# A two-layer fp32 model on one core: three gathered groups of tokens instead of two, and a routing step in another place

## The chip, the cores and the metric

The kernel runs on one core of a Trainium2 chip. The metric is the device time of one execution in microseconds (us). Engines are named as in the profile: PE (TensorE matmul), PEld (its weight loads), DVE (VectorE), ACT (ScalarE), POOL (GpSimd) and SP (SyncE, which here only issues transfers). DMA means the core's 16 DMA engines.

## The reference

The input is 512 tokens of width 1024, with 16 meta tokens ahead of them. The first block mixes them (convolution and latent attention) and then applies a feed-forward layer of experts. That layer is what the change touches:

```
q = (xb @ wq).reshape(C, 8 heads, 2, 64);  s = einsum('chpd,hpnd->chpn', q, keys)   # 128 keys per half
sv, si = top_k(s, 16)                                   # per head and half
top_s, sel = top_k((sv[:, :, 0, :, None] + sv[:, :, 1, None, :]).reshape(C, 8, 256), 16)
eidx = 16 of 128*128 experts per head;  g = softmax(top_s)
act = gelu(einsum('chkd,cd->chk', u_tab[eidx], xb))     # 8 * 16 = 128 experts per token
out = einsum('chk,chkd->cd', g * act, v_tab[eidx])
```

A second block follows (a gated convolution, a feed-forward layer, sparse attention, a feed-forward layer). All is computed in fp32 precision: a product of two fp32 matrices is made of three matmuls of high and low parts.

## The kernel before, in words

The layer of experts is computed in two ways. For the last 96 tokens the rows of `u_tab` and `v_tab` are **gathered** (groups of 64 and 32 tokens, `GROUPS`, line 60). For the other 416 (`TD`) it is computed **dense**: U times x for all 16384 experts, in 128 chunks of 128 experts, multiplied by a matrix G that holds the gates (zero for experts not chosen), and then V. A chunk of U is 24 matmuls of 128x128 weights and `TD` columns (lines 269 to 272); a V piece is 12 (lines 260 to 262), and a pass over half of a run's V is 8 pieces.

The order of the work on each engine is the order in which the program emits it (`manual_schedule`); nothing is planned by a tool.

**Stage A (352 to 830 us).** PE computes 84 chunks of U ahead (`ahead`), whose activations go to DRAM. Beside it DVE does the routing, a generator that yields charges; after each chunk it is advanced until the chunk's budget `BUD` is used up. The tokens lie in four tiles of 128, worked on in the order 3, 0, 1, 2. For each tile `route` ranks (`top16`, two heads at a time, 7.7 units, four times), decodes the indices to expert numbers (13.4 units), yields one more `BUD`, and lets PE transpose the result (`pt`, line 1078). For tile 3 it first computes `eg` and calls `pick` (line 921), which spreads the gathered tokens' indices and gates over the partitions. Then `onehots` builds one-hot matrices for 16 tokens on DVE (4 instructions, 6.7 units), and `build_g` multiplies them on PE, which ACT copies out and writes to `gd` in DRAM. There are `NSB` = 26 such blocks, 2 of them in tile 3. On ACT stand the casts of U to its high part (`wh`, line 119) and, in the decoding, an Exp; POOL subtracts to get the low part of U (`wl`, line 121).

**Gather steps.** `gstep` advances a second generator, `gathered`: each step loads one tile of 128 rows (512 KB) two steps ahead by an indirect DMA on POOL (line 935, three buffers), and takes one product on DVE: with x and a sum along the row for U (line 949), or times a factor and added to an accumulator for V (line 958). 64 tokens need 64 + 64 steps, 32 tokens 32 + 32. At the end of a group PE folds the accumulator (line 963). In stage A two chunks of six have a step, for which 1.9 units are charged.

**Stage B (850 to 1640 us).** 16 runs of 8 chunks. In each, G's part is loaded (`load_g`, POOL's queue), products and their high and low parts are made (`w_prod`, `w_split`), and two V passes follow (`v_pass`, accumulators `d`). Between the passes come the 44 fresh chunks of U, with one gather step each; `GV` lists after which of its 8 pieces a V pass takes a step. V is split by ACT and DVE two pieces ahead, with four buffers. What is left of the gather steps is done before the last V pass.

Of the kernel before, what the change touches and what calls it, by code (L numbers as in the profile page):

```python
# [9 lines left out]
F32 = mybir.dt.float32  # L10
# [33 lines left out]
AHEAD = 5  # L44
EXTRA = 4
PRE = 2
BUD = 5.0
NA = 4
NB = 1
ND = 2  # L50
# [39 lines left out]
OJ = (((), (0,), ()), ((1,), (), (2, 3)))  # L90
PF = 5
PA = tuple(range(6))
GV = (1, 2, 4, 6)


class Stream:
# [45 lines left out]
def _body(tc, nc, V, S, PE, GP, A, out, upto, tap, ctx):  # L142
# [99 lines left out]
    def col(name, i=0):  # L242
        p, n = COLS[name]
        return cols[:, p + i:p + i + 1]
# [100 lines left out]
    def xtile(p, h="xh", l="xl", n=8, c=T, bufs=None):  # L345
        return p.tile([128, n, c], F32R, name=h, bufs=bufs), p.tile([128, n, c], F32R, name=l, bufs=bufs)
# [429 lines left out]
    with ExitStack() as st:  # L776
        with st0 as st1:
            with ExitStack() as st2:
# [61 lines left out]
                xg = xq.tile([128, len(GROUPS), 8, 128], F32, name="xg")  # L840
# [20 lines left out]
                def norm_x(k):  # L861
                    tn = xq.tile([128, T], F32, name="tn", bufs=2)
                    V.scalar_tensor_tensor(tn, H[k], col("g_ffn", k), rB[:, :T], op0=OP.mult, op1=OP.mult)
                    split(xnh[:, k], xnl[:, k], tn, None)
                    for a, (t0, n, P) in enumerate(groups):
                        V.tensor_copy(xg[:, a, k].rearrange("p (b t) -> p b t", b=P),
                                      tn[:, None, t0:t0 + n].to_broadcast([128, P, n]))

                for h in range(8):
                    w = ws.get()  # L870
# [16 lines left out]
                for a, (t0, n, P) in enumerate(groups):  # L887
                    V.tensor_copy(dup[:, a].rearrange("p (b t) -> p b t", b=P),
                                  ident[:, None, t0 - 384:t0 - 384 + n].to_broadcast([128, P, n]))
                    xt.append(gx.tile([128, 1024], F32, name="xt", bufs=len(GROUPS)))  # L890
# [19 lines left out]
                S.activation(a, ps, AF.Gelu)  # L910
                return a

            gix = gx.tile([128, len(GROUPS), 64], U32, name="gix")
            gga = gx.tile([128, len(GROUPS), 64], F32, name="gga")
            gdt = gx.tile([128, len(GROUPS), 64], F32, name="gdt")

            def pick(eg):

                for a, (t0, n, P) in enumerate(groups):
                    ps = bank()  # L920
                    PE.matmul(ps[:, :256], lhsT=dup[:, a], rhs=eg.rearrange("p a n -> p (a n)"), start=True, stop=True)
                    m = 128 // P
                    for b in range(P):
                        r = slice(b * n, b * n + n)
                        V.tensor_copy(gix[r, a, :m], ps[r, b * m:b * m + m])
                        V.tensor_copy(gga[r, a, :m], ps[r, 128 + b * m:128 + b * m + m])

            def gathered():

                todo = [(a, v, j) for a, (t0, m, P) in enumerate(groups) for v in (0, 1) for j in range(128 // P)]  # L930
                tiles = []

                def load(a, v, j):
                    g = gx.tile([128, 1024], F32, name="row", bufs=GB)
                    GP.indirect_dma_start(out=g, out_offset=None, in_=A["vr" if v else "ur"],  # L935
                                          in_offset=bass.IndirectOffsetOnAxis(ap=gix[:, a, j:j + 1], axis=0))
                    tiles.append(g)

                for t in todo[:GB - 1]:
                    load(*t)  # L940
                yield
                for n, (a, v, j) in enumerate(todo):
                    if n + GB - 1 < len(todo):
                        load(*todo[n + GB - 1])
                    g = tiles.pop(0)
                    t0, m, P = groups[a]
                    L = 128 // P
                    if not v:
                        V.scalar_tensor_tensor(g, g, 1.0, xt[a], op0=OP.mult, op1=OP.mult,
                                               accum_out=gdt[:, a, j:j + 1])  # L950
                        if j == L - 1:
                            S.activation(gdt[:, a, :L], gdt[:, a, :L], AF.Gelu)
                            V.tensor_tensor(gdt[:, a, :L], gdt[:, a, :L], gga[:, a, :L], op=OP.mult)
                    elif j == 0:
                        gac[a] = gx.tile([128, 1024], F32, name="xt", bufs=len(GROUPS))
                        V.tensor_scalar(gac[a], g, gdt[:, a, 0:1], None, op0=OP.mult)
                    else:
                        V.scalar_tensor_tensor(gac[a], g, gdt[:, a, j:j + 1], gac[a], op0=OP.mult, op1=OP.add)  # L958
                    yield
                    if v and j == L - 1:  # L960
                        ps = bank()
                        for k in range(8):
                            PE.matmul(ps[:, k * m:(k + 1) * m], lhsT=gac[a][:, k * 128:(k + 1) * 128],
                                      rhs=fold[:, a, :m], start=True, stop=True)
# [3 lines left out]
            fold = gx.tile([128, len(GROUPS), 64], F32, name="fold")  # L968
            for a, (t0, n, P) in enumerate(groups):
                V.tensor_reduce(fold[:, a, :n], ident.rearrange("p (b t) -> p t b", b=P), op=OP.add, axis=AX.X)  # L970
            gat, gac = [], {}

            def gstep(n=1):
# [17 lines left out]
            def route(i):  # L991

                sv = wk.tile([128, 8, 2, 16], F32, name="sv", bufs=1)
                si = wk.tile([128, 8, 2, 16], U32, name="si", bufs=1)
                ts = wk.tile([128, 8, 16], F32, name="ts", bufs=1)
                tp = wk.tile([128, 8, 16], U32, name="tp", bufs=1)
                for h in range(0, 8, 2):
                    ch = []
                    for u in range(4):
                        tmp = wk.tile([128, 128], F32, name="tmp", bufs=4)  # L1000
# [17 lines left out]
                        ch.append((ts[:, h + u], tp[:, h + u], c, tmp[:, :112]))  # L1018
                    top16(ch)
                    yield 3.0  # L1020

                tpf = tp.rearrange("p h k -> p (h k)")
                ii = wk.tile([128, 8, 128], U32, name="ol")[:, :4]
# [42 lines left out]
                yield BUD  # L1066
                if i == 3:
                    eg = wk.tile([128, 2, 128], F32, name="eg", bufs=1)
# [61 lines left out]

# [29 lines left out]
        def load_g(r):  # L1160
            if r < len(runs):
                gt[r] = pk.tile([128, NSB, RUN, SUB], F32, name="gt", bufs=2)
                for b in range(0, NSB, NSB // GP_):
                    sl = slice(b, b + NSB // GP_)
# [740 lines left out]
```

## Time and profile before

| | |
|---|---|
| median of 3 runs | 2871.4 us (2870.38 to 2872.52) |
| the profiled execution | 2870.35 us, span 2868.2 us |
| PE busy | 2758.8 us (96%) in 14308 matmuls |
| DVE busy | 1905.4 us (66%) |
| ACT busy | 1193.5 us (42%) |
| POOL busy | 876.0 us (31%) |
| mean granted clock of PE | 0.982 |
| DMA | 457.17 MB, mean 159 GB/s |

The shares are means over stages with different limits. A matmul's end is modelled, so PE's pace is read from the distance between starts.

### The profile page before, as it was taken

To read this page: it belongs to the slowest core of one execution; us is meant where nothing else is said; L and a number is where in the kernel's file an instruction comes from. 1 tells how busy PE (TensorE), PEld (TensorE's weight loads), DVE (VectorE), ACT (ScalarE), POOL (GpSimd) and SP (SyncE) were. 2 spreads that over 40 slices of the span, in tenths; PEclk is the share of its full clock that TensorE was granted. 3 is DMA by queue.
4 is the path that set the end of the run, shared out by engine and by line. 5 is a ranking of instruction groups with operands and counts; after the bars stand their busy time and mean duration, and the time that the engine had idled before them with its cause. 6 is when DMAs were issued, how large, how long until landed. Compare 5 with 4: busy or idle time off the path is not lost. (4 is left out here: it accounts for less than half of the span.)

```text
span 2868.2 us, 38216 instructions
## 1 busy us (share of the span) xinstructions
PE 2758.8 (96%) x14308; PEld 2429.1 (85%) x14308; DVE 1905.4 (66%) x3477; ACT 1193.5 (42%) x1962; POOL 876.0 (31%) x521
## 2 busy tenths in 40 slices
PE   8778998999999999999999999999999999999998
PEld 7646898999989999999999988888887866788887
DVE  5887599798957867777778765444436489544433
ACT  5564543646553333343333423332223378433322
POOL 3653155555534456564456000000003133000000
PEclk9889999999999999999999999999999999999999
DMA  3102255767678888888888333333234200233332
GB/s 126 52 8 66 70 175 179 262 193 259 211 278 305 285 295 281 306 283 280 294 296 301 99 101 96 96 97 100 91 101 141 81 23 1 74 99 100 96 94 83
DMA packets 156568, 457.17 MB, mean 159 GB/s; under 512 B 17056, under 2 KB 40864, under 8 KB 152800
## 3 DMA queue, kind: packets, MB, share of 16 engines
q1 hardware_dynamic: 103008, 273.33, 29.5%
q0 software_dynamic: 36704, 135.54, 14.2%
q10 hardware_dynamic: 16672, 45.88, 4.0%
q8 instruction: 112, 1.84, 0.3%
q14 instruction: 72, 0.59, 0.1%
HBM read 407.43 MB, written 47.25 MB: 159 GB/s over the span
## 5 line engine op out<-in xcount | busy, mean ns | idle before, releaser
L119 ACT CAST wh<-wr 128x1024 fp32r<-128x1024 f32 (+1 forms) x356 | 369.4, 1038 | 394.4 <-issue 206.3
L121 DVE TENSOR_TENSOR wl<-wr,wh 128x1024 fp32r<-128x1024 f32 (+1 forms) x231 | 287.5, 1245 | 368.1 <-ACT wh L119 363.4
L121 POOL TENSOR_TENSOR wl<-wr,wh 128x1024 fp32r<-128x1024 f32 x125 | 334.0, 2673 | 330.2 <-ACT wh L119 325.4
L262 PE MATMUL m<-xh,wl 128*128 128x512 f32 x1080 | 422.2, 391 | 3.4 <-POOL wl L121 2.7
L260 PE MATMUL m<-xh,wh 128*128 128x512 f32 x1080 | 424.4, 393 | 0.0
L261 PE MATMUL m<-xl,wh 128*128 128x512 f32 x1048 | 407.9, 389 | 0.0
L269 PE MATMUL m<-xh,wh 128*128 128x416 f32 x1024 | 365.0, 356 | 9.7 <-ACT stg L1115 5.8
L261 PE MATMUL d<-wtl,vh 128*128 128x416 f32 x1024 | 359.5, 351 | 2.6 <-DVE wtl L253 2.6
L260 PE MATMUL d<-wth,vh 128*128 128x416 f32 x1024 | 359.8, 351 | 1.8 <-DVE hT L1206 0.9
L270 PE MATMUL m<-xl,wh 128*128 128x416 f32 x1024 | 360.9, 352 | 0.0
L262 PE MATMUL d<-wth,vl 128*128 128x416 f32 x1024 | 359.1, 351 | 0.2
L121 DVE TENSOR_TENSOR vl<-vr,vh 128x512 fp32r<-128x512 f32 x256 | 174.7, 688 | 140.1 <-ACT vh L119 133.9
L262 PEld LDWEIGHTS m<-xh,wl 128*128 128x128 f32 x1080 | 203.2, 188 | 49.4 <-DVE wl L121 3.4
L260 PEld LDWEIGHTS m<-xh,wh 128*128 128x128 f32 x1080 | 203.2, 188 | 43.3 <-issue 1.2
L119 ACT CAST vh<-vr 128x512 fp32r<-128x512 f32 x256 | 153.9, 619 | 206.1 <-DMA vr<-in_vr 148.5
L261 PEld LDWEIGHTS m<-xl,wh 128*128 128x128 f32 x1048 | 196.8, 188 | 41.2 <-issue 1.0
L935 POOL DMA_INDIRECT row<-in_vr,gix x96 | 174.6, 1818 | 141.0 <-DVE xt L958 109.3
L272 PE MATMUL m<-xh,wl 128*128 128x416 f32 x1024 | 213.3, 350 | 0.0
L910 ACT ACTIVATE act<-m 128x416 f32<-128x416 f32 x128 | 66.4, 519 | 343.3 <-PE m L272 336.5
L269 PEld LDWEIGHTS m<-xh,wh 128*128 128x128 f32 x1024 | 194.9, 190 | 15.8 <-ACT stg L1115 10.2
L261 PEld LDWEIGHTS d<-wtl,vh 128*128 128x128 f32 x1024 | 192.3, 188 | 5.5 <-DVE wtl L253 3.8
L260 PEld LDWEIGHTS d<-wth,vh 128*128 128x128 f32 x1024 | 192.2, 188 | 5.1 <-ACT act L910 1.3
(428 smaller groups left out, 5378.5 us busy)
## 6 DMA issues: line engine op xcount, KB each, us to landing
wr<-in_u SPq DMA_DIRECT2D x128, 512.0 KB
vr<-in_vr SPq DMA_DIRECT2D x256, 256.0 KB
wr<-in_w_gu SPq DMA_DIRECT2D x88, 512.0 KB
gd<-stg ACTq DMA_DIRECT2D x26, 1024.0 KB
gt<-gd POOLq DMA_DIRECT2D x32, 832.0 KB
ad<-act ACTq DMA_DIRECT2D x84, 208.0 KB
act<-ad SPq DMA_DIRECT2D x84, 208.0 KB
wr<-in_w_down SPq DMA_DIRECT2D x32, 512.0 KB
```

What stands on the lines that cost most here:

```text
L119: nc.scalar.copy(hi[:, :n], t[:, :n])
L121: eng.tensor_tensor(lo[:, :n], t[:, :n], hi[:, :n].bitcast(F32), op=OP.subtract)
L260: PE.matmul(ps, lhsT=wh, rhs=xh, start=first, stop=False)
L261: PE.matmul(ps, lhsT=wh, rhs=xl, start=False, stop=False)
L262: PE.matmul(ps, lhsT=wl, rhs=xh, start=False, stop=last)
L269: PE.matmul(ps, lhsT=wh, rhs=xhs[k], start=k == 0, stop=False)
L270: PE.matmul(ps, lhsT=wh, rhs=xls[k], start=False, stop=False)
L272: PE.matmul(ps, lhsT=w[1][:, wc + k * 128:wc + k * 128 + 128], rhs=xhs[k], start=False, stop=k == n - 1)
L910: S.activation(a, ps, AF.Gelu)
L935: GP.indirect_dma_start(out=g, out_offset=None, in_=A["vr" if v else "ur"], in_offset=bass.IndirectOffsetOnAxis(ap=gix[:, a, j:j + 1], axi ...
```

## The change

The tokens 400 to 415, dense before, form a third gathered group of 16 (P = 8: each token has 8 partitions, 16 + 16 more steps). `TD` is 400 and `NSB` 25; all matmuls of U and V have 400 columns. The third group's x is made late, inside the gather steps (`late_x`: eight products on DVE, eight transposes on PE, two copies on ACT), and `pick` folds its indices by a mask and seven adds, instead of copies from ranges of partitions. `GV` has five entries. `route` is cut in three: `rank`, `decode`, `turn`. The next tile's first ranking (heads 0 and 1) comes between a tile's `decode` and its `turn`, its other three after the tile's one-hots; the idle charge of one `BUD` after a decoding is 1.0. `BUD` is 4.9.

```diff
-BUD = 5.0
+BUD = 4.9
-GROUPS = ((64, 2), (32, 4))
+GROUPS = ((64, 2), (32, 4), (16, 8))
-GV = (1, 2, 4, 6)
+GV = (1, 2, 4, 5, 7)
...
-                xnh, xnl = xtile(xp)
+                xnh, xnl = xtile(xp, c=TD)
...
+                    if n % 32:
+                        x = wk.tile([128, 2, P, m], F32, name="o0", bufs=1)
+                        V.tensor_tensor(x, ps[:, :256].rearrange("p (z b j) -> p z b j", z=2, b=P),
+                                        own[:, None, :, None].to_broadcast([128, 2, P, m]), op=OP.mult)
+                        for b in range(1, P):
+                            V.tensor_tensor(x[:, :, 0], x[:, :, 0], x[:, :, b], op=OP.add)
+                        V.tensor_copy(gix[a], x[:, 0, 0])
+                        V.tensor_copy(gga[a], x[:, 1, 0])
+                        continue
...
+                def late_x(a):
+                    t0, m, P = groups[a]
+                    xs = gx.tile([128, 8, 128], F32, name="row", bufs=GB)
+                    for k in range(8):
+                        V.scalar_tensor_tensor(xs[:, k].rearrange("p (b t) -> p b t", b=P),
+                                               H[k][:, None, t0:t0 + m].to_broadcast([128, P, m]), col("g_ffn", k),
+                                               rB[:, None, t0:t0 + m].to_broadcast([128, P, m]),
+                                               op0=OP.mult, op1=OP.mult)
+                    xt.append(gx.tile([128, 1024], F32, name="xt", bufs=2))
+                    for z in range(2):
+                        ps = bank()
+                        for k in range(4):
+                            PE.transpose(ps[:, k * 128:(k + 1) * 128], xs[:, 4 * z + k], ident)
+                        S.copy(xt[a][:, 512 * z:512 * z + 512], ps)
...
                 for n, (a, v, j) in enumerate(todo):
+                    if len(xt) == a:
+                        late_x(a)
...
             def routing():
                 late = []
-                for i in (3, 0, 1, 2):
-                    tk = yield from route(i)
+                tiles = (3, 0, 1, 2)
+                yield from rank(3, range(0, 8, 2))
+                for n, i in enumerate(tiles):
+                    id01 = yield from decode(i)
+                    nxt = tiles[n + 1] if n < 3 else None
+                    if nxt is not None:
+                        yield from rank(nxt, (0,))
+                    tk = yield from turn(i, id01)
                     for s in range(min(8, NSB - 8 * i)):
                         a = yield from onehots(tk, s)
                         late.append((i, s) + a)
                         if len(late) > 1:
                             build_g(*late.pop(0))
+                    if nxt is not None:
+                        yield from rank(nxt, range(2, 8, 2))
```

## Rows read from the trace of the kernel before

**Rows 1.** Windows: length, busy of PE, PEld, DVE, ACT, POOL, PEclk, DMA share, GB/s.

```profile
488.00:622.00 134.00, 127.69 (x836) 123.63 (x835) 112.99 (x283) 71.50 (x87) 73.32 (x32) 0.98 0.67 227
900.00:1400.00 500.00, 499.92 (x2662) 495.81 (x2661) 368.29 (x521) 180.19 (x305) 277.79 (x161) 1.00 0.84 288
1400.00:1580.00 180.00, 180.00 (x958) 178.66 (x957) 140.31 (x198) 64.99 (x113) 95.34 (x53) 1.00 0.88 299
```

**Rows 2.** Waits of PE, 352:830: engine line <- releaser: us, times, longest.

```profile
PE m L1078 <- DVE id L1060: 9.6, 3, 4.9
...
PE m L269 <- ACT wh L119: 3.8, 2, 3.3
PE m L1113 <- ACT stg L1115: 2.8, 3, 2.3
PE m L921 <- DVE eg L1070: 2.4, 1, 2.4
PE m L1078 <- DVE id L1065: 2.3, 3, 1.6
```

**Rows 3.** Timeline of PE (start, length): steady 416, 512 and 256 columns.

```profile
1112.01 0.35 PE L261 MATMUL d<-wtl,vh 128*128 128x416 f32 x1
...
1113.90 0.35 PE L262 MATMUL d<-wth,vl 128*128 128x416 f32 x1
...
333.45 0.39 PE L260 MATMUL m<-xgh,wh 128*128 128x512 f32 x1
...
336.20 0.39 PE L260 MATMUL m<-xgh,wh 128*128 128x512 f32 x1
...
2840.84 0.28 PE L260 MATMUL m<-ah,wh 128*128 128x256 f32 x1
...
2841.42 0.28 PE L262 MATMUL m<-ah,wl 128*128 128x256 f32 x1
```

**Rows 4.** Groups by line: busy us, mean ns | idle before.

```profile
L269 PE MATMUL m<-xh,wh 128*128 128x416 f32 x1024 | 365.0, 356 | 9.7 <-ACT stg L1115 5.8 <-ACT wh L119 3.8
```

**Rows 5.** Timeline of DVE: a ranking's start and the next's, a decoding.

```profile
446.23 0.44 DVE L981 MAX8 ts<-cand 128x8 f32<-128x112 f32 x2
...
455.21 0.27 DVE L981 MAX8 ts<-cand 128x8 f32<-128x112 f32 x1
...
472.56 5.79 DVE L1059 TENSOR_TENSOR o<-o 128x1024 f16<-128x1024 f16 x3
478.38 0.29 DVE L1060 TENSOR_TENSOR id<-o 128x128 f32<-128x128 f16 x1
```

**Rows 6.** Timeline of POOL in that decoding.

```profile
475.34 2.40 POOL L121 TENSOR_TENSOR wl<-wr,wh 128x1024 fp32r<-128x1024 f32 x1 [0.55 <-ACT wh L119]
```

**Rows 7.** Timeline of PE: the pick matmuls.

```profile
408.81 2.08 PE L921 MATMUL m<-eg,dup 128*128 128x256 f32 x4 [2.45 <-DVE eg L1070]
```

**Rows 8.** Groups by line: the longest of the four one-hot instructions.

```profile
L1101 DVE TENSOR_TENSOR ol<-o,tk 128x2048 f16<-128x2048 f16 x26 | 47.1, 1812 | 0.0
```

**Rows 9.** Groups by line, DVE, 900 to 1600 us: a gather step.

```profile
L958 DVE SCALAR_TENSOR_TENSOR xt<-row,gdt,xt 128x1024 f32<-128x1024 f32 x94 | 127.4, 1355 | 6.3 <-DMA row<-in_vr,gix 6.2
```

**Rows 10.** Timeline of a V pass: DVE's split, PE's first use of it.

```profile
1111.92 0.69 DVE L121 TENSOR_TENSOR vl<-vr,vh 128x512 fp32r<-128x512 f32 x1
...
1113.33 0.35 PE L262 MATMUL d<-wth,vl 128*128 128x416 f32 x1
```

**Rows 11.** Timeline: transposes of x; before the last V pass, DVE and PE.

```profile
349.06 0.98 PE L893 MATMUL d<-ident,xg 128*128 128x128 f32 x7
...
1594.99 2.17 DVE L1206 TENSOR_TENSOR hT<-d,hT 128x832 f32<-128x832 f32 x2 [2.25 <-PE d L262]
...
1595.93 1.87 PE L963 MATMUL m<-fold,xt 128*128 128x32 f32 x16
```

**Rows 12.** Waits of POOL, 825 to 850 us.

```profile
POOL gt L1165 <- DMA gd<-stg: 24.2, 1, 24.2
```

**Rows 13.** Waits of PE, 850 to 900 us.

```profile
PE d L261 <- DVE wtl L253: 2.6, 4, 1.3
```

More of the change, by code (lines that the diff above doesn't have):

```diff
@@ L837, in _body @@
                     return dump()
-                xnh, xnl = xtile(xp)
+                xnh, xnl = xtile(xp, c=TD)
                 gx = pool(st, "gx", side="right")
-                xg = xq.tile([128, len(GROUPS), 8, 128], F32, name="xg")
+                xg = xq.tile([128, 2, 8, 128], F32, name="xg")
                 groups = []
@@ L863, in norm_x @@
                     V.scalar_tensor_tensor(tn, H[k], col("g_ffn", k), rB[:, :T], op0=OP.mult, op1=OP.mult)
-                    split(xnh[:, k], xnl[:, k], tn, None)
+                    split(xnh[:, k], xnl[:, k], tn[:, :TD], None)
                     for a, (t0, n, P) in enumerate(groups):
-                        V.tensor_copy(xg[:, a, k].rearrange("p (b t) -> p b t", b=P),
-                                      tn[:, None, t0:t0 + n].to_broadcast([128, P, n]))
+                        if a < 2:
+                            V.tensor_copy(xg[:, a, k].rearrange("p (b t) -> p b t", b=P),
+                                          tn[:, None, t0:t0 + n].to_broadcast([128, P, n]))
                 for h in range(8):
@@ L889, in _body @@
                                   ident[:, None, t0 - 384:t0 - 384 + n].to_broadcast([128, P, n]))
-                    xt.append(gx.tile([128, 1024], F32, name="xt", bufs=len(GROUPS)))
+                    if a == 2:
+                        break
+                    xt.append(gx.tile([128, 1024], F32, name="xt", bufs=2))
                     ps = bank("d")
@@ L911, in u_chunk, with parts @@
                 return a
-            gix = gx.tile([128, len(GROUPS), 64], U32, name="gix")
-            gga = gx.tile([128, len(GROUPS), 64], F32, name="gga")
-            gdt = gx.tile([128, len(GROUPS), 64], F32, name="gdt")
+            def parts(name, dt, sizes):
+                t = gx.tile([128, sum(sizes)], dt, name=name)
+                return [t[:, sum(sizes[:a]):sum(sizes[:a + 1])] for a in range(len(sizes))]
+            gix = parts("gix", U32, [128 // P for _, _, P in groups])
+            gga = parts("gga", F32, [128 // P for _, _, P in groups])
+            gdt = parts("gdt", F32, [128 // P for _, _, P in groups])
             def pick(eg):
@@ L935, in load @@
                     GP.indirect_dma_start(out=g, out_offset=None, in_=A["vr" if v else "ur"],
-                                          in_offset=bass.IndirectOffsetOnAxis(ap=gix[:, a, j:j + 1], axis=0))
+                                          in_offset=bass.IndirectOffsetOnAxis(ap=gix[a][:, j:j + 1], axis=0))
                     tiles.append(g)
+                def late_x(a):
[6 more added lines that the diff above has]
+                                               op0=OP.mult, op1=OP.mult)
+                    xt.append(gx.tile([128, 1024], F32, name="xt", bufs=2))
+                    for z in range(2):
[3 more added lines that the diff above has]
+                        S.copy(xt[a][:, 512 * z:512 * z + 512], ps)
                 for t in todo[:GB - 1]:
@@ L949, in gathered @@
                         V.scalar_tensor_tensor(g, g, 1.0, xt[a], op0=OP.mult, op1=OP.mult,
-                                               accum_out=gdt[:, a, j:j + 1])
+                                               accum_out=gdt[a][:, j:j + 1])
                         if j == L - 1:
-                            S.activation(gdt[:, a, :L], gdt[:, a, :L], AF.Gelu)
-                            V.tensor_tensor(gdt[:, a, :L], gdt[:, a, :L], gga[:, a, :L], op=OP.mult)
+                            S.activation(gdt[a], gdt[a], AF.Gelu)
+                            V.tensor_tensor(gdt[a], gdt[a], gga[a], op=OP.mult)
                     elif j == 0:
-                        gac[a] = gx.tile([128, 1024], F32, name="xt", bufs=len(GROUPS))
-                        V.tensor_scalar(gac[a], g, gdt[:, a, 0:1], None, op0=OP.mult)
+                        gac[a] = gx.tile([128, 1024], F32, name="xt", bufs=2)
+                        V.tensor_scalar(gac[a], g, gdt[a][:, 0:1], None, op0=OP.mult)
                     else:
-                        V.scalar_tensor_tensor(gac[a], g, gdt[:, a, j:j + 1], gac[a], op0=OP.mult, op1=OP.add)
+                        V.scalar_tensor_tensor(gac[a], g, gdt[a][:, j:j + 1], gac[a], op0=OP.mult, op1=OP.add)
                     yield
@@ L963, in gathered @@
                             PE.matmul(ps[:, k * m:(k + 1) * m], lhsT=gac[a][:, k * 128:(k + 1) * 128],
-                                      rhs=fold[:, a, :m], start=True, stop=True)
+                                      rhs=fold[a], start=True, stop=True)
                         h = hT[:, :, M0 + t0:M0 + t0 + m]
                         V.tensor_tensor(h, ps[:, :8 * m].rearrange("p (k t) -> p k t", k=8), h, op=OP.add)
-            fold = gx.tile([128, len(GROUPS), 64], F32, name="fold")
+            fold = parts("fold", F32, [n for _, n, P in groups])
             for a, (t0, n, P) in enumerate(groups):
-                V.tensor_reduce(fold[:, a, :n], ident.rearrange("p (b t) -> p t b", b=P), op=OP.add, axis=AX.X)
+                V.tensor_reduce(fold[a], ident.rearrange("p (b t) -> p t b", b=P), op=OP.add, axis=AX.X)
+            own = gx.tile([128, 8], F32, name="own")
+            V.tensor_reduce(own, ident.rearrange("p (b t) -> p b t", b=8), op=OP.add, axis=AX.X)
             gat, gac = [], {}
@@ L989, in top16, with rank @@
                     V.max_index(di[:, 8:16], dv[:, 8:16], tmp)
[L991 to L997, printed above, removed]
+            rk = {}
+            def rank(i, heads):
+                if 0 in heads:
+                    rk[i] = (wk.tile([128, 8, 2, 16], F32, name="sv", bufs=1),
+                             wk.tile([128, 8, 2, 16], U32, name="si", bufs=1),
+                             wk.tile([128, 8, 16], F32, name="ts", bufs=1),
+                             wk.tile([128, 8, 16], U32, name="tp", bufs=1))
+                sv, si, ts, tp = rk[i]
+                for h in heads:
                     ch = []
@@ L1065, in route, with turn @@
                 V.tensor_tensor(ge, ge, gs[:, 1, :, None].to_broadcast([128, 8, 16]), op=OP.mult)
-                yield BUD
+                yield 1.0
+                return id01
+            def turn(i, id01):
                 if i == 3:
-                    eg = wk.tile([128, 2, 128], F32, name="eg", bufs=1)
+                    eg = wk.tile([128, 8, 128], F32, name="o1")[:, :2]
                     V.scalar_tensor_tensor(eg[:, 0], id01[:, 0], 128.0, id01[:, 1], op0=OP.mult, op1=OP.add)
@@ L1162, in load_g @@
                 gt[r] = pk.tile([128, NSB, RUN, SUB], F32, name="gt", bufs=2)
-                for b in range(0, NSB, NSB // GP_):
-                    sl = slice(b, b + NSB // GP_)
+                m = -(-NSB // GP_)
+                for b in range(0, NSB, m):
+                    sl = slice(b, min(b + m, NSB))
                     nc.gpsimd.dma_start(gt[r][:, sl].rearrange("p b i t -> p b (i t)"),
```

6 lines of the change are left out of this document (4 added, 2 removed).

## The prediction

> **What bounds the kernel now.** I read the windows first, to see which engine is full in which stage. From 900 to 1400 us (V passes with fresh U chunks between them) PE is busy 499.92 of 500 us, and the same holds to 1580 [rows 1]: PE alone sets this stage, while DVE has a fifth to a quarter of its time free and the DMA engines are at 0.84 to 0.88. In the stage before (352 to 830 us: 84 ahead chunks of U beside the routing on DVE) PE has holes, 6.31 us in tile 1's period [rows 1]. PE's waits of that stage name them [rows 2]: transposes that wait for the decoding (9.6 + 2.3), a weight cast on ACT behind an Exp that waits for DVE (3.8), the last one-hot blocks (2.8), and the pick matmul for `eg` (2.4). Nothing after 1640 us is touched.
>
> **What 16 columns are worth.** In steady state matmuls with 416 columns start 1.89 us apart for 10 steps, 0.189 each; with 512 columns 2.75 for 12, 0.229; with 256 columns 0.58 for 5, 0.116 [rows 3]. Between 256 and 512 a column costs 0.44 ns, and 416 lies within 5 ns of that line; I take 6.85 ns for 16 columns (2.4 GHz alone gives 6.7). Six groups of 1024 such matmuls (one of them is [rows 4]) are 6144: 42.1 us of PE. The 44 fresh chunks of 24 and the 3072 matmuls of the V passes lie in the stage that PE fills: 4128 x 6.85 ns = **28.3 us** off the path. The 84 ahead chunks hold the other 13.8: a chunk falls from 24 x 0.188 = 4.52 us to 4.36.
>
> The Trainium skill (TensorE: Matmul & The Clock Gate, Back-to-back issue gap) has the spacing set by weight load and matmul together, 81 ns at N=128 and 131 at N=512; by that slope 16 columns would be an estimated 2.1 ns, and all 6144 matmuls worth 12.8 us. The trace's 0.229 us at 512 disagrees with that page, and the measurement decides.
>
> **The routing stage.** Tile 1's period of 134 us, less 24 chunks of 4.52, 4.5 of waits and 1 for transposes, leaves 2.5 us for each of its 8 one-hot blocks. PE's own work changes by -13.8 (columns), -2.5 (one block fewer) and +1.0 (a third pick matmul, by the 2.08 us of two [rows 7]): -15.3. But its waits change too; there I follow program order.
> - Tile 3. `eg` is computed in `turn`, so on DVE it now stands behind the ranking of tile 0's first two heads. Such a ranking took 8.98 us, with a gather step in it [rows 5]; I take 8.5. By the code's charges (52.9 units and five gather charges of 1.9, made although nothing is gathered yet, at 4.9 a chunk) the pick comes after 13 chunks instead of 12: PE arrives 13 x 4.36 - 12 x 4.52 = 2.4 us later. The wait for `eg`, 2.45 us [rows 7], becomes 2.45 + 8.5 - 2.4 = **8.6**, +6.1.
> - Tile 0 has the longest waits for decoding and cast, 4.9 + 3.3 = 8.2 [rows 2]. From pick to transposes PE has 12 chunks instead of 14 and a block: 13.4 less. DVE has one one-hot block less (four instructions of at most 1.8 us [rows 8], say 6), one ranking less (8.5), and 1.8 more to fold the third group (ten copies and adds, each under the 0.29 of a 128x128 add [rows 5]): 12.7 less. Then 8.2 + 13.4 - 12.7 = 8.9, +0.7.
> - Tiles 1 and 2 have the rest of those waits: 9.6 + 2.3 + 3.8 - 8.2 = 7.5. A tile now has 23 chunks between its transposes and the last ones, not 24. In tile 1's period DVE is busy 113 of 134 us [rows 1]; PE's work falls to 23 x 4.36 + 8 x 2.5 + 1 = 121. If the one-hots still wait for PE as today, the decoding is ready a ranking (8.5) earlier against a PE that comes some 6 earlier, and the waits fall to about 5. If DVE never waits in the one-hots any more, it starts the rankings some 6 us later against PE, and they grow to 18. The 8 us that DVE keeps free in a period are nearer to the second end: 16, +8.5.
> - Tail. The routing is charged 402.7 units of 84 x 4.9 and ends two chunks early, so the 2.8 us of the last blocks go: -3.
> Sum of the stage: -15.3 + 6.1 + 0.7 + 8.5 - 3 = **-3**. Ends: -16 (tiles 1 and 2 at their lower end, a ranking of 6.5) and +7 (each lag some 3 us longer).
>
> DVE's lag is partly POOL's doing: three half-adds of a decoding took 5.79 us, and POOL's subtraction ran meanwhile [rows 5, 6]. The Trainium skill (SBUF — State Buffer, SBUF: two separate sides) says that a DVE instruction with two SBUF inputs and a GpSimd one lock each other out for the whole instruction; the trace agrees with its 5.79 us. By it, shorter chunks bring the subtractions closer together and DVE gets no faster, which speaks against waits that vanish.
>
> **The V stage beside the columns.**
> - 32 more gather steps on DVE, 1.36 us each [rows 9], two more in a run of two passes. From 1400 to 1580 there are 8 passes: 140.3 + 8 x 1.36 = 151 in 8 x (17.4 + 4.36) = 174 us, 87%: covered by PE. Without that cover they cost 43 us.
> - DMA. 0.88 of 180 us at 299 GB/s is 340 GB/s when full; a row tile of 512 KB is 1.54 us. 158.4 + 8 x 1.54 - 1 (smaller G and activations) = 170 of 174 us, 97%; from 900 to 1400 it is 93%. The thin place is seen already: in a pass that starts with the load of G, the split of a V piece ends at 1112.61 and PE reads it at 1113.33 [rows 10], and PE will come 0.5 us sooner. Lower end 0 (the extra rows are asked for after that piece), upper end 32 x 1.54 = 49, if no gap of the DMA engines can be filled. Nearer to the lower row, as PE does not wait at all today: **+8**, most of it in the last four runs.
> - `late_x`: DVE adds the fold of group 1 first, which PE computes after its chunk; PE then waits for that add and eight products, 8 x 0.29 and 0.6, and does 8 transposes (7 took 0.98 us [rows 11]): **+4** (0 to 7).
> - A third fold of 1.87 us [rows 11]: **+1.9**.
> - Flush: three calls are left before the last pass instead of one. DVE adds the pass (to 1597.16 now), does two more steps of 1.36, to 1599.9, and PE was through at 1595.93 [rows 11]: **+4** (0 to 7).
> - The first run: POOL sits 24.2 us until the last block of G has landed [rows 12], and run 0's waits of PE (2.6 us for wtl [rows 13], and shorter ones) follow. With the blocks two chunks earlier: **-2.5** (-4.5 to 0).
> - `norm_x` splits 400 columns instead of 512, beside PE's matmuls: nothing; without cover under 0.2 us for each of eight.
>
> **Sum** against the profiled execution's own 2870.35 us (span 2868.2 and 2.15 around it): -28.3 - 3 + 8 + 4 + 1.9 + 4 - 2.5 = -15.9, so 2854.4; the median of the runs lies 1.05 higher: **2855.5**.
>
> **Rivals.**
> 1. The reordering works: with a ranking as buffer PE meets no late decoding at tiles 0 to 2. For it: 8.7 units of DVE work now lie between a decoding and its transposes in the order of emission. Against it: DVE's lag is as long, and the chunks are shorter. Then their 25 us of waits fall to about 8: 2855.5 - 17 = 2838.5.
> 2. The gathers' transfers take half of the V stage's gain: rows and V pieces share engines that are 93 to 97% used, and a V piece that comes late stops PE. For it: 0.7 us at the thin place; against it: PE has no wait in this stage today [rows 1]. 2855.5 + 12 = 2867.5.
> 3. The other side: the V stage becomes DMA-bound. From the point at which the idle 12 to 16% can't be filled, since a load waits until DVE has freed its buffer, the rows' 49 us replace the 8: 2855.5 + 41 = 2896; with half of the gaps filled, 2876.
> 4. The change doesn't give what it says: the weight load sets the pace, and 400 columns take as long as 416. Then 28.3 and some 8 of the routing stage stay: 2892. Against it: 0.116 us between starts at 256 columns, with weights of the same size [rows 3].
>
> **How the numbers follow.** Forecast 0.58, its own range 2846 to 2865; rival 1 0.13; rival 2 0.17; rival 3 0.08; rival 4 0.04. About 0.2% (5.7 us, what a measurement of this kernel can tell from no change) separates the signs: faster is the forecast, rival 1 and nearly half of rival 2, 0.78; within is the rest of rival 2 and the milder half of rival 3, 0.13; slower is what is left, 0.09. The range 2838 to 2870 leaves out rivals 3 and 4 and the far half of rival 1.
>
> **What would show it.** Right: starts 0.182 us apart in U chunks and V passes; a wait for `eg` near 8.6 us; waits at the transposes not gone; DMA near 0.95 in the late runs, with waits of PE of about a microsecond a run; some 4 us before the last pass. Wrong: starts that stay 0.188 apart; waits of PE above 2 us in each V pass; or waits at the transposes under 2 us in all, which would put the time below 2842.

## The result, and the profile after

The changed kernel takes 2911.8 us (median of 4 runs, 2908.9 to 2912.3) against 2872.0 (4 runs, 2870.4 to 2872.9) before: slower by 1.4%, ratio 1.014 with a 95% interval of 1.0127 to 1.0152. 2855.5 was forecast, with a range of 2838 to 2870: wrong in sign, and outside the range.

Three stretches of the profiled executions, cut at the first and the last matmul of the V stage, show where it went: 850.7, 764.9 and 1252.6 us before, 848.5, **809.3** and 1252.6 after. The stretch up to the V stage is 2.2 us shorter, near the 3 forecast, the rest is untouched, and the V stage grew by 44.4 us where it should have shrunk by some 13.

The windows of the changed kernel (columns as in [rows 1]):

```profile
488.00:622.00 134.00, 127.47 (x855) 123.39 (x854) 125.27 (x307) 71.75 (x88) 73.72 (x32) 0.99 0.68 226
900.00:1400.00 500.00, 474.92 (x2543) 469.66 (x2542) 381.61 (x525) 168.59 (x289) 288.63 (x175) 0.98 0.84 294
1400.00:1580.00 180.00, 173.41 (x927) 170.69 (x926) 143.03 (x204) 60.02 (x106) 101.74 (x60) 0.97 0.86 294
```

In the V stage PE is no longer full (474.9 of 500 us; 499.9 in [rows 1]), and its clock is below 1.00. No other engine has filled up in its place: DVE is busy 76 to 79%, and the DMA share is no higher than it was. PE's and then DVE's waits of the stage (860 to 1640 us) name what stops it:

```profile
PE d L262 <- DVE vl L121: 30.1, 12, 4.3
PE m L998 <- DVE xt L993: 3.9, 2, 3.7
PE d L260 <- ACT gdt L987: 3.5, 1, 3.5
```

```profile
DVE xt L993 <- DMA row<-in_vr,gix: 32.8, 12, 4.9
DVE row L984 <- DMA row<-in_ur,gix: 23.6, 17, 4.2
```

Twelve times PE waits for `vl`, the low half of a V piece, which DVE splits off. Eleven times DVE is late because it stands at a gather step whose row has not landed; the first time, at 880.71, it stands at G's own part for the run (6.66 us). DVE's waits for rows are 56.4 us in all, against 8.8 before (6.2 of them in [rows 9]):

```profile
DVE xt L958 <- DMA row<-in_vr,gix: 6.2, 9, 1.1
...
DVE row L949 <- DMA row<-in_ur,gix: 2.6, 3, 1.5
```

The wait of PE for `gdt` (3.5 us at 1584.37) has the same cause by another way: DVE stood 3.98 us at the last row of the third group's U, ACT's Gelu waits for that sum, and the next `vh` stands behind the Gelu on ACT.

The first pass of run 2 (the third of stage B's 16 runs) shows one such case on three engines. First POOL:

```profile
950.95 1.76 POOL L952 DMA_INDIRECT row<-in_ur,gix  x1 [0.16 <-issue]
952.72 2.28 POOL L1223 DMA_DIRECT2D gt<-gd  x2
955.30 1.00 POOL L952 DMA_INDIRECT row<-in_ur,gix  x1 [0.30 <-issue]
956.84 1.20 POOL L952 DMA_INDIRECT row<-in_ur,gix  x1 [0.54 <-DVE row L984]
958.59 1.14 POOL L952 DMA_INDIRECT row<-in_ur,gix  x1 [0.55 <-DVE row L984]
```

then DVE:

```profile
957.09 1.22 DVE L984 SCALAR_TENSOR_TENSOR row<-row,xt 128x1024 f32<-128x1024 f32 x1
...
964.16 0.69 DVE L121 TENSOR_TENSOR vl<-vr,vh 128x512 fp32r<-128x512 f32 x1 [5.24 <-ACT vh L119]
968.93 1.23 DVE L984 SCALAR_TENSOR_TENSOR row<-row,xt 128x1024 f32<-128x1024 f32 x1 [4.08 <-DMA row<-in_ur,gix]
970.08 0.08 DVE L984 DVE_READ_ACCUMULATOR row<-row,xt 128x1 f32 x1
970.08 0.69 DVE L121 TENSOR_TENSOR vl<-vr,vh 128x512 fp32r<-128x512 f32 x1
```

and PE:

```profile
966.98 0.34 PE L260 MATMUL d<-wth,vh 128*128 128x400 f32 x1
967.16 0.34 PE L261 MATMUL d<-wtl,vh 128*128 128x400 f32 x1
970.83 0.70 PE L262 MATMUL d<-wth,vl 128*128 128x400 f32 x1 [3.32 <-DVE vl L121]
971.33 0.54 PE L260 MATMUL d<-wth,vh 128*128 128x400 f32 x1
971.66 0.54 PE L261 MATMUL d<-wtl,vh 128*128 128x400 f32 x1
```

Read it from the cause on. The pass starts with the load of G, two transfers on POOL's queue (952.72, 1.6 MB). The row issued behind them at 955.30 is used only at 968.93, 13.6 us later; DVE has stood at it for 4.08 us, with the next piece's `vl` behind it in its queue. PE starts its last matmul before the stop at 967.16 and the next one at 970.83. From 971.33 its starts are 0.33 us apart, not 0.18. The windows around it show why:

```profile
966.00:971.00 5.00, 1.68 (x10) 1.32 (x9) 1.88 (x4) 2.00 (x4) 0.56 (x1) 0.87 1.02 396
971.30:976.40 5.10, 5.10 (x17) 5.06 (x17) 5.10 (x5) 0.51 (x1) 3.81 (x3) 0.50 0.96 332
```

For the 5 us after the stop the granted clock is 0.50, the 1.2 GHz level. So this late row is paid twice: by the stop, and by a stretch at half speed. Not every one is. After eight of the twelve stops for `vl` (1.8 to 4.3 us) the clock of the next 3 to 5 us is 0.50 to 0.66; after the other four (1.3 to 2.9 us, at 1079.65, 1182.69, 1234.19 and 1385.83) it stays at 1.00, as here:

```profile
1234.60:1239.60 5.00, 5.00 (x30) 5.00 (x28) 5.00 (x4) 0.66 (x1) 3.92 (x3) 1.00 1.00 366
```

What tells the two kinds apart was not tested.

The whole V stage can be counted so, from the starts of its 4007 matmuls of 400 (416) columns: steady spacing times 4007; what gaps (over 0.45 us from start to start) have beyond a steady spacing; what slow starts (0.22 to 0.45) have beyond it; and the other matmuls (folds, transposes). In us:

| kernel | steady | gaps | slow starts | other | V stage | whole, median |
|---|---|---|---|---|---|---|
| before | 754.5 (0.1883 each) | 5.2 | 1.9 | 3.4 | 764.9 | 2872.0 |
| changed | 730.1 (0.1822 each) | 49.2 | 20.1 | 9.8 | 809.3 | 2911.8 |

### The profile page after: what moved, and what is told of

Same layout as the page of the kernel before. It is cut to its first block, busy times and chain, and to the rows that moved or that the text cites. A ratio compares the mean times of both kernels' runs of the same rounds, so it can differ in the third digit from the quotient of the medians.

```text
span 2910.5 us, 38356 instructions
## 1 busy us (share of the span) xinstructions
PE 2754.2 (95%) x14302; PEld 2421.8 (83%) x14302; DVE 1969.3 (68%) x3544; ACT 1184.6 (41%) x1961; POOL 920.5 (32%) x553
## 5 line engine op out<-in xcount | busy, mean ns | idle before, releaser
L262 PE MATMUL d<-wth,vl 128*128 128x400 f32 x1024 | 359.1, 351 | 30.4 <-DVE vl L121 30.1
L269 PE MATMUL m<-xh,wh 128*128 128x400 f32 x1024 | 363.0, 354 | 13.1 <-ACT wh L119 7.3
L260 PE MATMUL d<-wth,vh 128*128 128x400 f32 x1024 | 359.2, 351 | 7.6 <-ACT gdt L987 3.5
L261 PE MATMUL d<-wtl,vh 128*128 128x400 f32 x1024 | 359.0, 351 | 2.1 <-DVE wtl L253 2.1
L270 PE MATMUL m<-xl,wh 128*128 128x400 f32 x1024 | 358.5, 350 | 0.0
L952 POOL DMA_INDIRECT row<-in_vr,gix x112 | 187.5, 1674 | 171.9 <-DVE xt L993 128.4
L262 PEld LDWEIGHTS d<-wth,vl 128*128 128x128 f32 x1024 | 197.0, 192 | 37.2 <-DVE vl L121 36.6
L272 PE MATMUL m<-xh,wl 128*128 128x400 f32 x1024 | 208.9, 346 | 0.2
L913 ACT ACTIVATE act<-m 128x400 f32<-128x400 f32 x128 | 64.7, 505 | 333.3 <-PE m L272 333.2
```

Of the source, the lines that this page charges most:

```text
L260: PE.matmul(ps, lhsT=wh, rhs=xh, start=first, stop=False)
L261: PE.matmul(ps, lhsT=wh, rhs=xl, start=False, stop=False)
L262: PE.matmul(ps, lhsT=wl, rhs=xh, start=False, stop=last)
L269: PE.matmul(ps, lhsT=wh, rhs=xhs[k], start=k == 0, stop=False)
L270: PE.matmul(ps, lhsT=wh, rhs=xls[k], start=False, stop=False)
L272: PE.matmul(ps, lhsT=w[1][:, wc + k * 128:wc + k * 128 + 128], rhs=xhs[k], start=False, stop=k == n - 1)
```

## The experiments

**Theory Q**: rows issued behind G's load in POOL's queue land too late for DVE, which works in order, and the V piece behind them stops PE. Theory S: the shorter passes alone do it. Theory V: the volume of the rows does it, wherever they stand. For the routing stage, theory D: DVE sets its pace, so the order of its work brings little. Fourteen kernels, each timed in 3 rounds beside the kernel before (2871.4 to 2871.8 in these).

**1. The fifth step alone.** Before, with one line of the change:

```diff
-GV = (1, 2, 4, 6)
+GV = (1, 2, 4, 5, 7)
```

> The kernel before with the fifth gather step per V pass alone (GV = 1, 2, 4, 5, 7; still 96 tokens, 416 columns). Theory Q (a gather row queued behind the load of G lands late, DVE waits for it in order, and the V split behind it comes late): waits of PE of 1 to 3 us in each pass that starts with the load of G until the steps are used up (run 12), 2885 to 2900 us. Rival S (it is the shorter matmuls that use up the 0.3 to 1.5 us that V pieces 6 and 7 had): no waits here, 2872 us.

Measured: 2890.6 us, ratio 1.0068 (1.0051 to 1.0084). Gaps in its V stage 26.8 us, slow starts 7.6. Its waits in the V stage:

```profile
DVE xt L958 <- DMA row<-in_vr,gix: 19.4, 14, 3.4
...
DVE row L949 <- DMA row<-in_ur,gix: 13.2, 11, 5.4
```

```profile
PE d L262 <- DVE vl L121: 16.9, 11, 4.5
```

The old pace of 416 columns and no third group, and the same wait is there: five steps in a pass are enough. Theory S is out as the only cause; the shorter passes can only add to it. The profiled execution was the slowest of the four, 2899.6 us, so these waits may be more than the median's.

**2. The change without the third group's gathering.** It leaves out the gathered part of 16 tokens.

```diff
-GV = (1, 2, 4, 5, 7)
+GV = (1, 2, 4, 6)
...
-todo = [(a, v, j) for a, (t0, m, P) in enumerate(groups) for v in (0, 1) ...
+todo = [(a, v, j) for a, (t0, m, P) in enumerate(groups[:2]) for v in (0, 1) ...
```

> The kernel after without the 32 gather steps of the third group and with GV = 1, 2, 4, 6; the gathered part of 16 tokens is left out. Theory Q: V stage without waits, 28 us of columns gained and 3 in the routing: 2840 us. Rival S: the waits at pieces 6 and 7 stay at 2 to 3 us a run, 2885 us or more.

Measured: 2850.2 us, 0.9926 (0.991 to 0.9943); V stage 750.2 us, waits of DVE for rows 4.0. That is 10 us above the 2840 expected, a miss of the size: the steady spacing gives the V stage 24.4 us, and gaps, slow starts and other matmuls take 9.6 of them back. But PE has no stop for `vl` left: the loss of the change hangs on the added gather steps.

**3. G on another queue, with the same bytes.**

```diff
-nc.gpsimd.dma_start(gt[r]...
+(nc.scalar if r > 1 else nc.gpsimd).dma_start(gt[r]...
```

> The kernel after with the loads of G of runs 2 to 15 issued from ACT's queue instead of POOL's, same bytes. Theory Q (order within POOL's queue): the rows no longer stand behind G, PE's waits in the V stage fall from some 49 us to under 15, and the half-clock stretches behind them go too: about 2860 us. Rival V (the 16 DMA engines are full, whichever queue): no change, 2905 to 2915 us, or worse as G then competes with the V pieces.

Measured: 2869.9 us (10 runs), 0.9999 (0.9989 to 1.0009): 42 us less than the changed kernel, for a transfer issued from another engine. DVE's and PE's waits in the V stage:

```profile
DVE xt L993 <- DMA row<-in_vr,gix: 17.7, 17, 2.4
DVE row L984 <- DMA row<-in_ur,gix: 9.9, 12, 2.2
```

```profile
PE d L262 <- DVE vl L121: 1.8, 3, 1.3
```

Theory V (no change) is out: most of the loss is the place behind G. The 2860 that I expected was not reached; 27.6 us of waits for rows are left, the longest 2.4 us. The edit moves two things for the row behind G: its place in the queue, and its issue, which in the first pass of run 2 comes 1.3 us after the first matmul instead of 3.6, because POOL no longer spends 2.28 us on issuing G. The landings under run 13 show the first by itself.

**4. `eg` before the moved ranking**, so that the pick doesn't wait behind it.

```diff
+if i == 3:  # at the end of decode
+    eg3.append(...)
+    V.scalar_tensor_tensor(eg3[0][:, 0], ...); V.tensor_copy(eg3[0][:, 1], ...)
...
-eg = ...; pick(eg)
+pick(eg3[0])
```

> The kernel after with eg computed before the next tile's ranking, not behind it. Theory D (DVE sets the pace of the routing stage): the wait for eg falls from 9.6 us to 1 or 2, but tile 0's waits at cast and transposes grow by nearly the same, and the time stays within 3 us of 2911.8. Rival (the wait was simply added): 9 us faster, 2903 us.

Measured: 2909.0 us (2898.2 to 2915.1), 1.013 (1.0101 to 1.0159). PE's waits of the routing stage (352 to 830 us), the changed kernel first:

```profile
PE m L928 <- DVE o L1119: 9.7, 1, 9.7
PE m L1127 <- DVE id L1105: 9.5, 3, 3.4
PE m L269 <- ACT wh L119: 7.3, 3, 3.7
...
PE m L1127 <- DVE id L1110: 2.3, 3, 1.6
```

and with `eg` first:

```profile
PE m L1128 <- DVE id L1105: 8.3, 3, 3.4
PE m L269 <- ACT wh L119: 7.3, 3, 3.7
PE m L269 <- DVE gga L943: 5.4, 1, 5.4
...
PE m L928 <- DVE o L1114: 2.3, 1, 2.3
```

The wait for `eg` goes from 9.7 to 2.3, and 5.4 of it is back a moment later, at the copies that follow the pick. The whole stays within 3 us, but its four runs scatter too widely to exclude the rival's 2903. The end of the stage decides for theory D: the first V matmul starts at 847.9 us, 0.6 earlier than in the changed kernel, not 9.

**5. The change with the old routing order.**

```diff
-yield from rank(3, range(0, 8, 2))
 for n, i in enumerate(tiles):
+    yield from rank(i, range(0, 8, 2))
     id01 = yield from decode(i)
-    nxt = tiles[n + 1] if n < 3 else None
-    if nxt is not None:
-        yield from rank(nxt, (0,))
+    yield BUD - 1.0
...
-    if nxt is not None:
-        yield from rank(nxt, range(2, 8, 2))
```

> The changed kernel with the routing order of before (each tile ranked whole, decoded, then turned); 112 tokens and everything else stay. Theory D (VectorE sets the pace of the routing stage, so the order of its work brings next to nothing): first V matmul within 3 us of the changed kernel's 848.5, whole 2908 to 2916 us. Rival (the new order hides the decoding): without it the routing stage is 8 to 17 us longer, 2920 to 2929 us.

Measured: 2908.2 us, 1.0127 (1.011 to 1.0144); first V matmul at 845.3 us, 848.5 with the new order. The reordering, one of the two halves of the change, brings nothing (in these profiles, 3 us the wrong way). PE's waits only change their names: `eg` 4.6, transposes 7.4 + 1.3, casts 10.0.

**6. The kernel before with G on ScalarE's queue**, by the edit of run 3.

> The kernel before (96 tokens, four steps per pass) with the loads of G from run 2 on issued from ScalarE's queue instead of GpSimd's. Theory Q (rows late behind G only matter where VectorE then waits, and before VectorE waited 8.8 us for rows and TensorE's gaps in the V stage sum to 5.6 us): 2866 to 2873 us, at most 5 us off. Rival (G ahead of the rows costs in any schedule): 10 to 20 us off, 2852 to 2862 us.

Measured: 2871.5 us, 1.0005 (0.9995 to 1.0014). Four steps a pass already had their rows in time, so the queue costs nothing there: a late row has a price only from the point where it eats the lead of the V pieces.

**7 and 8. G in five parts, spread over the pass**, from ScalarE's queue and from POOL's.

```diff
+GJ = (0, 1, 2, 4, 5)
-load_g(r + 1)
-v_pass(r, 0, ...)
+v_pass(r, 0, ... {j: [(load_gp, (r + 1, 5 * n, 5 * n + 5))] for n, j in enumerate(GJ)})
```

> The changed kernel with each G load of runs 2 and later cut in five parts of five sub-blocks, issued after pieces 0, 1, 2, 4 and 5 of the pass from ScalarE's queue. Theory B (what is left with G on ScalarE's queue is the burst: 1.6 MB at once delays rows and V pieces): VectorE's waits for rows fall below 15 us from 27.6, whole 2856 to 2866 us. Rival (the volume of rows, not their order): 2868 to 2873 us as with G on ScalarE's queue in one go.

> As the run with G in five parts after pieces 0, 1, 2, 4 and 5, but issued from GpSimd's queue as in the changed kernel. Theory Q in its form 'a row waits for the bytes that stand ahead of it in its queue': a part is a fifth of the bytes, a row waits about 2 us instead of 9, and most of the loss goes: 2862 to 2880 us. Rival (any G load on GpSimd's queue holds it up, whatever its size): 2895 to 2912 us.

Measured: 2867.5 us, 0.9987 (0.9977 to 0.9997), and 2865.2 us, 0.9979 (0.997 to 0.9989). Spreading does as much on POOL's own queue as another queue does. For run 7 I was wrong: its waits for rows were to fall under 15 us and are 43.4, and its time lies above the 2856 to 2866 expected. The waits of run 8 are the surprise:

```profile
DVE xt L994 <- DMA row<-in_vr,gix: 40.0, 32, 2.7
...
DVE row L985 <- DMA row<-in_ur,gix: 26.4, 19, 3.0
```

```profile
PE d L261 <- DVE hT L1271: 3.7, 7, 1.0
PE d L263 <- DVE vl L122: 1.1, 4, 0.4
```

DVE waits longer for rows than in the changed kernel (66.4 us against 56.4), in 51 waits instead of 29, and yet PE's waits for `vl` fall from 30.1 to 1.1 us. So the sum of DVE's waits does not decide. The longest goes with the loss (3.0 against 4.9 us); that it is the lead of the V pieces that covers the short ones is argued, the lead itself was not measured.

**9. G in five parts, all issued at once.**

```diff
-GP_ = 2
+GP_ = 5
```

> The changed kernel with G's load cut in five parts instead of two, but all five issued together at the start of the pass from GpSimd's queue, as the changed kernel issues its two. Theory Q (what counts is the bytes that stand ahead of a row in its queue): no change, 2905 to 2914 us. Rival (small loads let the rows in between, whatever the place of the issue): most of the loss goes as in the run with the parts spread over the pass (2865.2), 2865 to 2880 us.

Measured: 2900.1 us, 1.0105 (1.0088 to 1.0123). Some 12 us better, so below theory Q's range and far above the rival's: both miss, but PE still waits 23.0 us for `vl`, DVE up to 4.6 us for a row, and most of the loss stays. In 15 of the 16 loads the row behind G lands 1.8 to 3.0 us after G's last part, so all of G's bytes still stand ahead of it. Why PE loses less is not shown.

**10 and 11. No steps left for the last pass; G over two passes.** Run 8 with a sixth step in the second pass of six runs, and then with three of G's parts moved to the second pass of the run before.

```diff
-if j in GV:
+if j in GV or j == 3 and h == 1 and r in GX:   # GX = (1, 3, 5, 7, 9, 11)
...
+GJ1 = ((1, 0), (4, 5), (6, 10))    # run 11: second pass of the run before
+GJ0 = ((1, 15), (4, 20))           # run 11: first pass
```

> The run with G in five parts on GpSimd's queue (2865.2 us), with one more gather step after piece 3 of the second pass of runs 1, 3, 5, 7, 9 and 11, so that no steps are left for the last pass. Theory (of what is left, the wait ahead of the last fold, a gap of 5.2 us at 1584, is the largest piece): the gap goes, 2858 to 2862 us. Rival (six more steps in second passes make V pieces late there): 2865 to 2870 us.

> As the run with no steps left for the last pass, and G's five parts spread over two passes (after pieces 1, 4 and 6 of the second pass of the run before and after pieces 1 and 4 of the first pass). Theory Q: with fewer bytes ahead of any row, VectorE's waits for rows fall from 66 us to under 40, and TensorE's small gaps at the start of passes with them: 2853 to 2860 us. Rival (the 16 DMA engines are nearly full, 89% of their time in these queues, so spreading more gives nothing): 2858 to 2864 us, as without.

Measured: 2872.5 us, 1.0006 (0.9996 to 1.0016), and 2865.5 us, 0.9977 (0.9968 to 0.9987). Run 10 is a miss: the wait before the last fold falls from 5.0 to 1.2 us, but the sixth step delays DVE's add at the end of those passes, and PE waits for it:

```profile
PE d L262 <- DVE hT L1272: 11.7, 9, 3.6
```

Run 11 brings waits for rows down to 38.5 us as expected, but the gaps in the passes remain (`hT` 10.1 us), so that both edits together end where run 8 was; its time is a miss too (2853 to 2860 expected).

**12. A fourth row buffer on top of run 11.**

```diff
+if "pk" in big and big["n"] % 4 == 0:
+    g = big["pk"].tile([128, 1024], F32, name="row4", bufs=1)
...
-if n + GB - 1 < len(todo):
-    load(*todo[n + GB - 1])
+while nxt < len(todo) and nxt < n + GB + ("pk" in big):
+    load(*todo[nxt]); nxt += 1
...
-name="act", bufs=6
+name="act", bufs=5
```

> As the run with G over two passes, with a fourth buffer for rows in the V stage (paid for by one of the six buffers for activations), so that a row is issued three steps ahead of its use instead of two. Theory Q: waits for rows fall below 15 us, and the V stage to 748 to 755 us from 763.7; whole 2848 to 2857 us. Rival (the DMA engines are full, or activations come late with five buffers): no better than with three buffers, within 3 us of it.

Measured: **2853.4 us**, 0.9941 (0.9925 to 0.9958): faster than both kernels. No wait of DVE for a row's transfer is left in the stage (the one wait at a row that remains is for ACT's copy in `late_x`), though rows and G are as many bytes as in the changed kernel, in less time. DVE's waits and the windows:

```profile
DVE hT L1010 <- PE m L1007: 8.7, 3, 4.4
...
DVE row L993 <- ACT xt L977: 1.2, 1, 1.2
```

```profile
900.00:1400.00 500.00, 500.00 (x2753) 499.98 (x2752) 395.68 (x574) 182.96 (x312) 329.30 (x224) 1.00 0.90 323
1400.00:1580.00 180.00, 179.22 (x987) 178.25 (x986) 143.43 (x216) 66.34 (x116) 93.35 (x64) 0.99 0.84 297
```

PE is full again, at clock 1.00 and a DMA share of 0.90. So the DMA engines were not the limit of the changed kernel.

**13. The fourth buffer alone**, G as in the changed kernel.

> The changed kernel with only the fourth row buffer of the V stage (five activation buffers instead of six); G stays in two loads at the start of the pass on GpSimd's queue. Theory Q in the form 'a row is late because it is issued only two steps ahead of its use, behind G': one step more (about 3 us) takes the longest wait for a row from 4.9 us to about 2, which the lead of the V pieces covers: 2862 to 2880 us. Rival (behind 1.6 MB a row is late whatever its lead): 2895 to 2912 us.

Measured: 2870.8 us, 0.9997 (0.9987 to 1.0007), 41 us less than the changed kernel. One step more of lead does what moving G does: the row issued behind G at 955.69 is used at 968.45, by a DVE that never waited for it:

```profile
955.69 1.10 POOL L956 DMA_INDIRECT row<-in_ur,gix  x1 [0.30 <-issue]
```

```profile
967.84 0.69 DVE L121 TENSOR_TENSOR vl<-vr,vh 128x512 fp32r<-128x512 f32 x1
968.45 1.22 DVE L990 SCALAR_TENSOR_TENSOR row<-row,xt 128x1024 f32<-128x1024 f32 x1
```

The landings, which this trace records, show what the row had waited for. G's second transfer (issued 954.29) and this row, with KB and us from issue to landing:

```profile
gt<-gd POOLq DMA_DIRECT2D x1, 768.0 KB, 11.0
...
row<-in_ur,gix POOLq DMA_INDIRECT x1, 11.5
```

The row landed at 967.2, 1.9 us after G; in 15 of this run's 16 loads the distance is 1.8 to 2.0 us. In run 6, with G on ScalarE's queue, the second transfer of G (issued 949.25) and the next row (issued 953.92):

```profile
gt<-gd ACTq DMA_DIRECT2D x1, 832.0 KB, 14.7
...
row<-in_ur,gix POOLq DMA_INDIRECT x1, 8.2
```

Here the row landed 1.8 us before G, and so in all ten loads from ScalarE's queue whose landing is recorded, by 1.0 to 8.1 us. That a row need not wait for G once G stands in another queue agrees with the Trainium skill (DMA: Bandwidth & Descriptors, Queues, rings and completion order), by which each DMA engine takes turns between the queues that it has work for. So in run 13 the rows are still late behind G, and the fourth buffer gives the lead that covers it.

**14. The kernel before with two neighbouring steps.**

```diff
-GV = (1, 2, 4, 6)
+GV = (1, 2, 4, 5)
```

> The kernel before (96 tokens, four steps per pass) with the last step moved from after piece 6 to after piece 5, so that two steps stand next to each other, as in the changed kernel. Theory of the place (two neighbouring steps in the pass with G use a row before it can have landed, whatever the number of steps): slower, 2878 to 2892 us. Rival, theory of the number (only the fifth step empties the lead of the rows): no change, 2868 to 2875 us.

Measured: 2878.3 us, 1.0025 (1.0015 to 1.0034). The place of the steps alone costs 7 of the 19 us of run 1, with 5.5 us of waits for `vl`; the rest, by subtraction, goes with the fifth step itself. Neither theory was the whole.

The V stages counted as above, in us. They are counts of the profiled executions, which lie within 2.4 us of the medians, but for run 1 (2899.6, 9 above):

| run | gaps | slow starts | other | V stage | whole, median |
|---|---|---|---|---|---|
| 1 before, five steps | 26.8 | 7.6 | 3.4 | 792.4 | 2890.6 |
| 2 no third group's gathering | 9.5 | 5.5 | 5.1 | 750.2 | 2850.2 |
| 3 G on ScalarE's queue | 17.8 | 10.3 | 9.7 | 767.8 | 2869.9 |
| 8 G spread, POOL's queue | 18.3 | 5.7 | 9.7 | 763.7 | 2865.2 |
| 12 spread and fourth buffer | 8.4 | 4.1 | 8.0 | 750.4 | 2853.4 |
| 13 fourth buffer alone | 17.3 | 8.9 | 9.1 | 765.2 | 2870.8 |

## Why the prediction was wrong

**The step that failed** is the DMA term, "Nearer to the lower row, as PE does not wait at all today: **+8**", with "upper end 32 x 1.54 = 49". Gaps and slow starts together rose from 7.1 to 69.3 us; less 3.8 before the last fold and 1.1 around `late_x`, which had terms of their own, some 57 us stand where 8 were, beyond the upper end too. Three things were wrong in it.

- It priced bandwidth: bytes over what 16 engines move, averaged over windows. What counted was one row's time from issue to use, 13.6 us behind G, against the two steps of lead that three buffers give it. Averaged, the DMA share never rose ([rows 1] against the windows above); while the row of 955.30 was under way it was nearly full:

```profile
955.30:968.90 13.60, 12.21 (x68) 11.85 (x66) 4.31 (x8) 2.48 (x4) 3.34 (x3) 1.00 0.96 324
```

- "The extra rows are asked for after that piece" (the lower end) looked at the V piece's own transfer. In the pass shown ACT had cast the piece by 966.77; its split on DVE began at 970.08, behind a row. I had [rows 10], with 0.7 us between DVE's `vl` and PE's use, and read it as a matter of transfers. The right question was what stands before `vl` in DVE's queue, and how late that can become.
- The price of a stop left out the clock: 18.2 us of the loss (20.1 less 1.9) are slow starts, some 15 of them behind the twelve stops for `vl` and most of the rest behind the stops at `late_x`, `gdt` and the last fold.

Of the rivals, number 2 ("a V piece that comes late stops PE") had the wait and 12 us for it; number 3 was the side on which it ended, though beyond its 2896, and half its mechanism: run 12 moves the rows and fills PE, so the stage is not bound by the DMA engines, but its reason, "a load waits until DVE has freed its buffer", is what the fourth buffer takes away. The prediction's own sign of being wrong, "waits of PE above 2 us in each V pass", came in part: twelve stops for `vl` in 32 passes, at most one in a run, eight of them above 2 us.

**The steps that held.**

- Columns: starts 0.1822 us apart, 0.182 forecast; 0.1883 before, so 6.1 ns for 16 columns where I took 6.85. Over 4007 matmuls that is 24.4 us, where 28.3 were forecast over 4128. Rival 4 is out.
- Routing stage: the first V matmul comes 2.2 us earlier, -3 was forecast. The wait for `eg` is 9.7 us (8.6), transposes and casts of tiles 0 to 2 take 19.1 (9.5 + 2.3 + 7.3; 8.9 + 16 = 24.9 forecast), the last blocks 1.0 instead of 2.8. That the sum fits is in part luck: PE's waits up to 830 us rose from 27.3 to 35.9, 8.6 where the terms add up to 12.3, so that PE's own work fell by some 10.8 us, not by 15.3. Rival 1 is out, by runs 4 and 5 too: DVE, at 125 of 134 us in tile 1's period, sets the pace as far as these runs show, and the waits only move.
- DVE's 32 steps more are covered: run 12 does them all, and its PE is full.
- `late_x` and the third fold, +5.9 forecast: the other matmuls rose by 6.4 and the waits by 1.1. The flush, +4: a gap of 3.8 us.

So with the rows in time the change is worth three quarters of what the other terms say: they add up to -23.9, and run 12, which has no flush either, lies 18 us under the kernel before. That its 2853.4 is near the 2855.5 forecast is luck: that sum is made of other terms.

**What stays open.** Runs 3, 8 and 13 each win back 41 to 47 us by different means and stop at V stages of 764 to 768 us; run 11 is at 761, and only with more lead, a spread G and no flush together does it fall to 750. How much of the last 14 us belongs to which was not separated. Open too are why run 9 loses less than the changed kernel, and why the clock falls after some stops only. The first run's -2.5 us cannot be told from the shifts of a few us that the first V matmul shows between kernels.

## What to carry to other kernels

Before adding transfers to a queue, list what each one will stand behind, and compare its time from issue to landing with its lead in steps; the mean share of the DMA engines (0.84 before and after) did not show it here. Then ask what stands behind the waiting instruction on its own engine: an item that is off the critical path stops the path when a critical one follows it in order. Where a lead is short, one buffer more or the large load cut up and spread gave back nearly all of the loss, and the longest wait was a better sign of it than the sum of the waits.

## What the runs showed of the hardware

- After eight of the twelve stops for `vl` (1.8 to 4.3 us) PE ran at a granted clock of 0.50 to 0.66 for the next 3 to 5 us, with starts 0.33 us apart; after four (1.3 to 2.9 us) it ran on at 1.00. The stops' own 44 us more than before came with 18 us of slow starts more.
- A row tile of 512 KB issued on POOL's queue behind 1.6 MB was used 13.6 us later in the changed kernel. Such a row landed 1.8 to 2.0 us after G's last transfer in 15 of 16 loads of run 13, and before it, by 1.0 to 8.1 us, in the ten loads of run 6 from ScalarE's queue. With the same bytes on two queues, or with the load in parts along the pass, the longest wait for a row fell from 4.9 us to 2.4 and 3.0.
- In the kernel before, the three half-adds of a decoding on DVE took 1.47 us with POOL idle (484.31) and 5.79 us while POOL subtracted (472.56).
